# A two-layer encoder on one core: seven first-stage tiles with k outermost, x by chunks, the squares' adds on VectorE and the first norm ahead of the last chunk's products

## The chip, the cores and the metric

The kernel runs on one core of one Trainium2 chip. The metric is the time of one execution on the device in microseconds (us); less is better. A profiled execution also has a span, from its first to its last instruction. TensorE (PE) multiplies matrices, VectorE (DVE), ScalarE (ACT) and GpSimd (POOL) work element by element, and SyncE (SP) issues DMA transfers. PEld is TensorE's weight load, which runs beside its matmuls.

## The reference

All arrays are float32. `x` is 256 tokens of width 1024. Each of two layers computes, from `h = rms_norm(x)`, one wide product `h @ w_in`, whose columns feed three mixers and their gates: latent attention ("a": latents of 256 and 128 columns and a rotary part of 32), dilated attention ("b") and neighbourhood attention ("c": q, k and v of 8 heads of 64). The mixers' outputs are gated, go through an output product and are added to `x`; then comes a SwiGLU feed-forward of width 2816 on a second norm. A last norm ends the kernel. Cut to what bears on the change:

```python
def rms_norm(x, g):
    xf = x.astype(jnp.float32)
    y = xf * lax.rsqrt(jnp.mean(xf * xf, axis=-1, keepdims=True) + EPS)
    return (y * g.astype(jnp.float32)).astype(x.dtype)
...
    q = (rms_norm(c_q, g_q) @ w_uq).reshape(B, S, MLA_HEADS, MLA_NOPE_DIM + MLA_ROPE_DIM)
    kv = (rms_norm(c_kv, g_kv) @ w_ukv).reshape(B, S, MLA_HEADS, MLA_NOPE_DIM + MLA_V_DIM)
```

The norm's factor is a number per token, so the kernel multiplies the plain `x * g` with the weights and applies the factor `RB` to the products afterwards. The latents `c_q` and `c_kv` have norms of their own, which must be finished before their products with `w_uq` and `w_ukv` can start.

## The kernel before, in words

**Layout.** Channels lie on the 128 partitions, so `x` is 8 chunks of 128 channels by 256 tokens in `X`. Every float32 operand is used as a rounded part and a remainder: `prep` makes `XH` (ACT) and `XL` (DVE) of a chunk of `x * g`. A weight chunk is loaded by SP into a `raw` buffer (6 buffers, five chunks ahead), `split_next` makes `hi` of it on ACT and `lo` on DVE (4 buffers each), and `mm3` uses it in three matmuls of 256 columns a tile: hi with XH, hi with XL, lo with XH. `plan` fixes the order of the weight chunks, and `take` hands out the next one and starts the split of the one after it.

**First stage (key "a").** For each k of the 8 channel chunks: `prep`, one weight chunk of 640 columns, and five tiles' products, 15 matmuls; two of the tiles are the first half of the neighbourhood keys ("ck"). After every second chunk `square_pair` squares two chunks on ACT; POOL adds the squares up. After the loop `rstd` sums them over the channels (matmuls into `ps_ss`), takes the inverse root (`newton`, on ACT and DVE), and spreads it over the partitions (`ps_r`, then a copy into `RB`). Then `cq`, `ckv` and their squares are made, the other two "ck" tiles are multiplied (`n_tile`, 24 matmuls each), and the latent norm follows: sums in `ps_n`, `newton_wide` (two Ln and one Exp on ACT; two multiplications and a last step on DVE, lines 378 to 380), multiplications on POOL (L729, L730), then `chl`: rounded part on ACT (L735), remainder on DVE (L736). Four "cq" tiles, a "cv" tile and "cvk" products lie beside it; they do not need `chl`. `latent_q` (chunks "uq") and `latent_kv` ("ukv") do. After them `latent_rope` makes 16 small multiplications on DVE (L764), and six "b" q tiles come next.

**Feed-forward start.** `residual`, `prep` of two chunks, one "f" weight chunk, `square_pair` and 24 matmuls into `ps_f`, four times; `lo` of the first "f" chunk is made on POOL, all others on DVE.

**Order.** The code names no order across tiles: the framework simulates the program when it is built and orders each engine's instructions by readiness and free buffers. So the order within an engine changes where code, sizes or engines change; each engine then runs its list strictly in order. Matmuls of several stages stand mixed in TensorE's list.

Of the kernel before, what the change touches and what calls it, by code (L numbers as in the profile page):

```python
# [18 lines left out]
S = 256  # L19
NL = 2  # L20
KC = D // P
# [74 lines left out]

def plan():

    out = [(("a", k), 640) for k in range(KC)]
    out += [(("ck", i), 1024) for i in (2, 3)] + [(("cq", i), 1024) for i in range(4)]  # L100
    out += [(("uq", 0), 768)] + [(("cv", 0, h), 1024) for h in range(2)] + [(("uq", 1), 768)]
    for k, n in LAST:
        out += [(("cvk", k, n), 288 * n)] + [(("ukv",), 1024)] * (k == 0)
    out += [(("b", "q", i), 1024) for i in range(6)]
    out += [(("bv", 0, q), 1024) for q in range(4)] + [(("bv", 2, h), 1024) for h in range(2)]
    out += [(("b", "k", i), 1024) for i in range(6)]
    out += [(("g", j, br), 1024) for j in range(8) for br in range(3)]
    for j in range(10):
        if j < 8:
            out += [(("mab", j), 768), (("mc", j), 512)]  # L110
        if j > 1:
            out += [(("o", j - 2), 1024)]
    out += [(("f", c), 1024) for c in range(4)]
    for f in range(2, NF):
        out += [(("w1", f), 1024), (("w3", f), 1024)]
        if f > 2:
            out += [(("w2", f - 3), 1024)]
    out += [(("w2", f), 1024) for f in range(NF - 3, NF)]
    return out
# [6 lines left out]
def pack_weights(i, l):  # L126
# [17 lines left out]
    def part(key):  # L144
        n = key[0]
        if n == "a":
            c = np.concatenate([np.arange(384), nb_heads("ck", 0), nb_heads("ck", 1)])
            return w_in[P * key[1] : P * key[1] + P, c]
        if n in ("ck", "cq"):
            return tiles(w_in, nb_heads(n, key[1]))  # L150
        if n == "cvk":
            c = np.concatenate([OFF_C + 1280 + np.arange(256), 384 + n32])
# [40 lines left out]
    out = []  # L193
# [38 lines left out]
def f32(ap):  # L232
    return ap.bitcast(F32)
# [3 lines left out]
def encoder(ctx: ExitStack, tc: tile.TileContext, x, w, gains, cst, rpb, gfin, out):  # L237
# [52 lines left out]
    def split_next():  # L290
        i = at["split"]
        width = chunks[i][2]
        t = raw.pop(i)
        hi = ring.tile([P, 1024], F32R, tag="hi", name="hi", bufs=4)
        lo = ring.tile([P, 1024], F32R, tag="lo", name="lo", bufs=4)
        act.copy(hi[:, :width], t[:, :width])  # L296
        eng = pool if chunks[i][1] == ("f", 0) else dve
        ins = eng.tensor_sub(lo[:, :width], t[:, :width], f32(hi[:, :width])).ins  # L298
        if eng is dve and "hold" in at:
            queue(ins, at["hold"])  # L300
        split[i] = (hi, lo)
        at["split"] += 1
# [100 lines left out]
    def square_pair(c2):  # L403
        xs = X[:, 2 * c2 : 2 * c2 + 2, :].rearrange("p c s -> p (c s)")
        if c2 == 0:
            t = tmp.tile([P, 2, 512], F32, tag="qb", name="sqs", bufs=1)
            sqs["t"] = t[:, 0, :]
            act.activation(sqs["t"], xs, AF.Square)
        else:
            q = tmp.tile([P, 512], F32, tag="t2k", name="sq", bufs=4)  # L410
            act.activation(q, xs, AF.Square)
            pool.tensor_add(sqs["t"], sqs["t"], q)

    def sums(ps, at, sq, n, col, start):

# [197 lines left out]
    if True:  # L613
# [5 lines left out]
        for i in range(10):  # L619
            mm(wb, warm[:, :P], warm, True, True)  # L620
        act.dma_start(G, gains)
        ahead(0, 1)
        sp.dma_start(X[:, 1, :], x[:, 1, :])
        for c2 in range(1, 4):
            ahead(0, c2 + 1)
            sp.dma_start(X[:, 2 * c2 : 2 * c2 + 2, :], x[:, 2 * c2 : 2 * c2 + 2, :])

        def load_consts(n):
            return sp.dma_start(C[:, CPARTS[n] : CPARTS[n + 1]], cst[:, CPARTS[n] : CPARTS[n + 1]])
# [17 lines left out]
        for l in range(NL):  # L647

            gq, gk = bank("pv", "ps_g"), bank("pv", "ps_g")
            pc = [bank("g", "ps_g"), bank("g", "ps_g")]  # L650
            for k in range(KC):
                prep(k, GM + 8 * l)
                wt = take(l, "a", k)
                if k % 2:
                    square_pair(k // 2)
                for n in range(5):
                    o = (gq, gk, pc[0])[(n + n // 3) // 2][:, cols((n + n // 3) % 2, S)]
                    mm3(o, wt, cols(n), XH[:, k, :], XL[:, k, :], k == 0 and n in (0, 2, 3), k == 7)
            if l == 0:
                load_consts(0)  # L660
            rstd()


            QA = tmp.tile([P, 8, S], F32, tag="qa", name="QA", bufs=1)
# [46 lines left out]
                    stack(v, [QC[e][:, n, :] for e in range(2)], [v.bitcast(F32R)] * 2, "lo")  # L711

            c_out("k", 0, pc[0])
            for i in range(2):
                n_tile(l, pc[1][:, cols(i, S)], ("ck", 2 + i))
            c_out("k", 1, pc[1])
            if l == 0:
                braw = bias_tile()
# [272 lines left out]
            for c2 in range(4):  # L991
# [5 lines left out]
                for kk in range(2):  # L997
                    k = 2 * c2 + kk
                    for n in range(4):
                        mm3(fb[n // 2][:, cols(n % 2, S)], wt, slice(kk * 512 + n * P, kk * 512 + n * P + P),  # L1000
                            XH[:, k, :], XL[:, k, :], k == 0 and n % 2 == 0, k == 7)

            def swiglu(o):
                ab = tmp.tile([P, 2, S], F32, tag="t2k", name="fab", bufs=4)
                dve.tensor_mul(ab, o.rearrange("p (n s) -> p n s", n=2), bc(RB, 2))  # L1005
                halves["s"] = 4 - halves.get("s", 0)
                s = SG[:, halves["s"] : halves["s"] + 3, :]
                fn(s[:, 0, :], ab[:, 0, :], AF.Sigmoid)
                pool.tensor_mul(s[:, 1, :], ab[:, 0, :], ab[:, 1, :])  # L1009
                dve.tensor_mul(s[:, 2, :], s[:, 1, :], s[:, 0, :])  # L1010
                lag.append(in_halves(s[:, 2, :]))
# [123 lines left out]
```

## Time and profile before

| | us |
|---|---|
| median of 3 runs | 920.01 |
| the runs | 917.07, 920.01, 2275.41 |
| the profiled execution | 919.51 |
| its span | 917.7 |

The profiled execution's time is 1.8 us more than its span and 0.5 us under the median of the runs. The mean granted TensorE clock is 0.996 of full speed. Busy time is the time in which an engine had an instruction under way; the sum of a group's durations can be larger where instructions overlap. For matmuls that follow one another, the distance of their starts is the price of one, and not the duration shown, which has the pipeline's fill in it.

### The profile page before, as it was taken

To read this page: it belongs to the slowest core of one execution; us is meant where nothing else is said; L and a number is where in the kernel's file an instruction comes from. 1 tells how busy PE (TensorE), PEld (TensorE's weight loads), DVE (VectorE), ACT (ScalarE), POOL (GpSimd) and SP (SyncE) were. 2 spreads that over 40 slices of the span, in tenths; PEclk is the share of its full clock that TensorE was granted. 3 is DMA by queue.
4 is the path that set the end of the run, shared out by engine and by line. 5 is a ranking of instruction groups with operands and counts; after the bars stand their busy time and mean duration, and the time that the engine had idled before them with its cause. 6 is when DMAs were issued, how large, how long until landed. Compare 5 with 4: busy or idle time off the path is not lost.

```text
span 917.7 us, 18370 instructions
## 1 busy us (share of the span) xinstructions
PE 903.4 (98%) x7350; PEld 864.8 (94%) x7350; DVE 660.2 (72%) x1003; ACT 520.2 (57%) x858; POOL 127.4 (14%) x138
## 2 busy tenths in 40 slices
PE   8999999999999999999999999999999999999996
PEld 6999899999999999999999979999999999999995
DVE  6989876555888666666699898665577976666663
ACT  6687974544656444444477789545355654444443
POOL 2223013000022100000023230400000210000000
PEclk9999999999999999999999999999999999999998
DMA  8985455444666765665377654543456566555531
GB/s 284 292 280 187 135 154 173 118 136 144 203 205 199 260 207 185 190 190 187 110 239 213 222 159 137 154 139 133 129 182 219 166 211 203 185 184 189 197 120 46
DMA packets 53030, 166.70 MB, mean 182 GB/s; under 512 B 6352, under 2 KB 7120, under 8 KB 52944
## 3 DMA queue, kind: packets, MB, share of 16 engines
q1 hardware_dynamic: 48384, 158.69, 53.8%
q0 software_dynamic: 1920, 3.15, 1.6%
q10 hardware_dynamic: 2640, 3.69, 1.1%
q8 instruction: 58, 0.95, 0.4%
q14 instruction: 28, 0.23, 0.1%
HBM read 157.64 MB, written 1.05 MB: 173 GB/s over the span
## 4 chain that ended last, share of the span: by engine, by line
PE 93%; DVE 4%; ACT 1%; DMA 1%; issue 0%; SPq 0%; DVEq 0%
PE ps_g L322 63%; PE ps_acc L322 16%; PE ps_s L322 3%; PE ps_y L322 3%; PE ps_t L522 2%; PE ps_c L322 2%; DVE lo L298 2%; PE ps_f L322 1%; PE ps_a L322 1%; DVE XL L399 1%; DMA X<-in_x 1%; ACT hi L296 1%; DVE t L975 0%; DVE X L987 0%; PE ps_r L322 0%
## 5 line engine op out<-in xcount | busy, mean ns | idle before, releaser
L296 ACT CAST hi<-raw 128x1024 fp32r<-128x1024 f32 (+5 forms) x308 | 304.3, 993 | 311.6 <-PE ps_g L322 160.2
L298 DVE TENSOR_TENSOR lo<-raw,hi 128x1024 fp32r<-128x1024 f32 (+4 forms) x306 | 372.8, 1226 | 143.2 <-ACT hi L296 142.2
L322 PE MATMUL ps_g<-XH,hi 128*128 128x256 f32 x1392 | 392.2, 283 | 1.1 <-ACT hi L296 1.1
L322 PE MATMUL ps_g<-XL,hi 128*128 128x256 f32 x1392 | 389.6, 281 | 0.0
L322 PE MATMUL ps_g<-XH,lo 128*128 128x256 f32 x1392 | 386.3, 280 | 1.6 <-DVE lo L298 1.6
L322 PEld LDWEIGHTS ps_g<-XH,hi 128*128 128x128 f32 x1392 | 261.8, 188 | 5.4 <-issue 1.9
L322 PEld LDWEIGHTS ps_g<-XL,hi 128*128 128x128 f32 x1392 | 262.2, 188 | 3.2 <-issue 2.3
L322 PEld LDWEIGHTS ps_g<-XH,lo 128*128 128x128 f32 x1392 | 260.4, 188 | 2.4 <-DVE lo L298 2.2
L322 PE MATMUL ps_acc<-HL,hi 128*128 128x256 f32 x608 | 109.3, 280 | 0.0
L322 PEld LDWEIGHTS ps_acc<-HL,hi 128*128 128x128 f32 x608 | 93.1, 188 | 0.0
L322 PE MATMUL ps_acc<-HL,lo 128*128 128x256 f32 x304 | 84.2, 279 | 0.0
L1009 POOL TENSOR_TENSOR SG<-fab 128x256 f32<-128x256 f32 x44 | 34.5, 786 | 305.7 <-DVE fab L1005 302.5
L322 PEld LDWEIGHTS ps_acc<-HL,lo 128*128 128x128 f32 x304 | 57.1, 188 | 0.0
L322 PE MATMUL ps_acc<-hi,HL 128*128 128x512 f32 x176 | 55.3, 395 | 0.0
L1005 DVE TENSOR_TENSOR fab<-ps_g,RB 128x512 f32<-128x512 f32 x40 | 27.6, 691 | 22.2 <-PE ps_g L322 22.2
L322 PE MATMUL ps_g<-hi,XH 128*128 128x256 f32 (+2 forms) x128 | 40.4, 316 | 0.0
L322 PE MATMUL ps_g<-hi,XL 128*128 128x256 f32 (+2 forms) x128 | 40.0, 313 | 0.0
L322 PE MATMUL ps_g<-lo,XH 128*128 128x256 f32 (+2 forms) x128 | 39.9, 315 | 0.0
L322 PEld LDWEIGHTS ps_acc<-hi,HL 128*128 128x128 f32 x176 | 31.7, 188 | 6.1
L322 PE MATMUL ps_acc<-lo,HL 128*128 128x512 f32 x88 | 34.8, 395 | 0.0
L532 ACT COPY pT<-ps_t 128x512 f32<-128x512 f32 (+1 forms) x48 | 26.1, 549 | 14.1 <-PE ps_t L522 13.8
L926 DVE TENSOR_TENSOR GL<-ps_g,RB 128x512 f32<-128x512 f32 x20 | 13.8, 692 | 24.0 <-PE ps_g L322 24.0
(194 smaller groups left out, 1247.1 us busy)
## 6 DMA issues: line engine op xcount, KB each, us to landing
raw<-in_w SPq DMA_DIRECT2D x250, 512.0 KB, 3.6
raw<-in_w SPq DMA_DIRECT2D x20, 384.0 KB, 3.1
raw<-in_w SPq DMA_DIRECT2D x16, 320.0 KB, 3.3
braw<-in_rpb SPq DMA_DIRECT2D x16, 256.0 KB, 5.1
raw<-in_w SPq DMA_DIRECT2D x16, 256.0 KB, 2.8
t<-t ACTq DMA_DIRECT2D x24, 128.0 KB, 3.2
raw<-in_w SPq DMA_DIRECT2D x4, 432.0 KB, 4.2
KCt<-KCt POOLq DMA_DIRECT2D x8, 128.0 KB, 5.1
```

The source lines that it names most:

```text
L296: act.copy(hi[:, :width], t[:, :width])
L298: ins = eng.tensor_sub(lo[:, :width], t[:, :width], f32(hi[:, :width])).ins
L322: pe.matmul(o, a, b, start=start, stop=stop, skip_group_check=True)
L399: dve.scalar_tensor_tensor(out=XL[:, c, :], in0=X[:, c, :], scalar=g, in1=f32(XH[:, c, :]), op0=ALU.mult, op1=ALU.subtract)
L522: pe.transpose(u.tr[:, cols(k)], u.p[:, cols(k)], cc("ident"))
L532: act.copy(u.pT[:, :n], u.tr[:, :n])
L926: dve.tensor_mul(d0[:, n0 : n0 + 2, :], o.rearrange("p (n s) -> p n s", n=2), bc(RB, 2))
L1005: dve.tensor_mul(ab, o.rearrange("p (n s) -> p n s", n=2), bc(RB, 2))
L1009: pool.tensor_mul(s[:, 1, :], ab[:, 0, :], ab[:, 1, :])
```

## The change

The change makes the first stage's chunk 896 columns wide, with all four "ck" tiles in it: seven tiles and 21 matmuls a chunk, and no separate "ck" tiles after it. The second "ck" bank comes from the tag "acc". `x` is loaded in single chunks of 128 KB, each after a weight chunk's transfer; the constants are asked for at k = 3 and not after the loop. The adds of the squares go to DVE as one function, `add_squares`; `rstd` is called before the last chunk's products are emitted; at the feed-forward `add_squares` is called after the loop. `lo` of the first "f" chunk is made on DVE.

```diff
@@ def plan
-    out = [(("a", k), 640) for k in range(KC)]
-    out += [(("ck", i), 1024) for i in (2, 3)] + [(("cq", i), 1024) for i in range(4)]
+    out = [(("a", k), 896) for k in range(KC)]
+    out += [(("cq", i), 1024) for i in range(4)]
...
@@ def split_next
-        eng = pool if chunks[i][1] == ("f", 0) else dve
-        ins = eng.tensor_sub(lo[:, :width], t[:, :width], f32(hi[:, :width])).ins
-        if eng is dve and "hold" in at:
+        ins = dve.tensor_sub(lo[:, :width], t[:, :width], f32(hi[:, :width])).ins
+        if "hold" in at:
...
@@ def square_pair
-            sqs["t"] = t[:, 0, :]
+            sqs["t"], sqs["more"] = t[:, 0, :], []
             act.activation(sqs["t"], xs, AF.Square)
         else:
             q = tmp.tile([P, 512], F32, tag="t2k", name="sq", bufs=4)
             act.activation(q, xs, AF.Square)
-            pool.tensor_add(sqs["t"], sqs["t"], q)
+            sqs["more"].append(q)
+
+    def add_squares():
+        for q in sqs["more"]:
+            dve.tensor_add(sqs["t"], sqs["t"], q)
...
@@ the loads of x
-        ahead(0, 1)
-        sp.dma_start(X[:, 1, :], x[:, 1, :])
-        for c2 in range(1, 4):
-            ahead(0, c2 + 1)
-            sp.dma_start(X[:, 2 * c2 : 2 * c2 + 2, :], x[:, 2 * c2 : 2 * c2 + 2, :])
+        for c in range(1, KC):
+            ahead(0, min(c, 6))
+            sp.dma_start(X[:, c, :], x[:, c, :])
...
@@ the first stage
-            pc = [bank("g", "ps_g"), bank("g", "ps_g")]
+            pc = [bank("g", "ps_g"), bank("acc", "ps_g")]
             for k in range(KC):
                 prep(k, GM + 8 * l)
                 wt = take(l, "a", k)
+                if l == 0 and k == 3:
+                    load_consts(0)
                 if k % 2:
                     square_pair(k // 2)
-                for n in range(5):
-                    o = (gq, gk, pc[0])[(n + n // 3) // 2][:, cols((n + n // 3) % 2, S)]
-                    mm3(o, wt, cols(n), XH[:, k, :], XL[:, k, :], k == 0 and n in (0, 2, 3), k == 7)
-            if l == 0:
-                load_consts(0)
-            rstd()
+                if k == KC - 1:
+                    add_squares()
+                    rstd()
+                for n in range(7):
+                    o = (gq, gk, *pc)[(n + (n > 2)) // 2][:, cols((n + (n > 2)) % 2, S)]
+                    mm3(o, wt, cols(n), XH[:, k, :], XL[:, k, :], k == 0 and n in (0, 2, 3, 5), k == 7)
...
             c_out("k", 0, pc[0])
-            for i in range(2):
-                n_tile(l, pc[1][:, cols(i, S)], ("ck", 2 + i))
             c_out("k", 1, pc[1])
...
@@ the feed-forward, after the loop over c2
+            add_squares()
```

**How the order moves.** DVE at the latent norm of layer 0, before (the `nw` and `R_` rows are `newton_wide`; `lo` rows split weight chunks, told apart by width: 1024 for "cq", "cv" and "ukv", 768 for "uq", 864 and 576 for "cvk"):

```order
L378 TENSOR_TENSOR nw<-nw,R_427 128x512
L710 SCALAR_TENSOR_TENSOR cv<-ps_g,RB 128x512
L379 TENSOR_TENSOR nw<-nw,R_427 128x512
L298 TENSOR_TENSOR lo<-raw,hi 128x1024
L380 SCALAR_TENSOR_TENSOR R_427<-nw,R_427 128x512
L439 TENSOR_TENSOR cv<-cv,QC 64x512 x2
```

And the same place now:

```order
L377 TENSOR_TENSOR nw<-nw,R_418 128x512
L442 TENSOR_TENSOR cv<-cv,QC 64x512 x2
L378 TENSOR_TENSOR nw<-nw,R_418 128x512
L442 TENSOR_TENSOR cv<-cv,QC 64x512 x2
L297 TENSOR_TENSOR lo<-raw,hi 128x864
L379 SCALAR_TENSOR_TENSOR R_418<-nw,R_418 128x512
```

Four remainders of the "cq" tiles and an 864-wide split now stand inside the three steps of the latent norm; a multiplication and one 1024-wide split stood there before.

ACT at the same place, before and now (the `R_` rows are the norm's Ln, Ln and Exp):

```order
L344 ACTIVATE R_427<-ps_n,C 128x256
L296 CAST hi<-raw 128x768
L344 ACTIVATE R_427<-ps_n,C 128x256
L344 ACTIVATE R_427<-R_427 128x512
L296 CAST hi<-raw 128x1024
```

```order
L343 ACTIVATE R_418<-ps_n,C 128x256 x2
L296 CAST hi<-raw 128x768
L343 ACTIVATE R_418<-R_418 128x512
L441 CAST QC<-cv 64x512 x4
L296 CAST hi<-raw 128x864
```

The 768-wide cast was that of "uq" 0 and stood between the two Ln; now it is that of "uq" 1, behind both and ahead of the Exp.

TensorE where `chl` is first read, before and now, with buffer numbers (`hi_549` is "uq" 0, `hi_589` a "cv" chunk; now `hi_540` is "uq" 0, `hi_640` "uq" 1, `hi_673` the first "cvk"):

```order
L322 MATMUL ps_g_617<-hi_589,XH_68 128x256
L322 MATMUL ps_a_596<-chl_437,hi_549 128x256
L322 MATMUL ps_r_588<-chl_437,hi_549 128x256
L322 MATMUL ps_g_617<-hi_589,XL_69 128x256
L322 MATMUL ps_g_617<-lo_590,XH_68 128x256
```

```order
L321 MATMUL ps_g_717<-hi_673,XL_69 128x288
L321 MATMUL ps_g_717<-lo_674,XH_68 128x288
L321 MATMUL ps_a_587<-chl_428,hi_540 128x256
L321 MATMUL ps_r_579<-chl_428,hi_540 128x256
L321 MATMUL ps_a_680<-chl_428,hi_640 128x256
L321 MATMUL ps_g_718<-hi_673,XH_68 128x288
```

The first reader of `chl` stood among the "cv" products; now it stands behind all of them and behind nine "cvk" matmuls.

DVE at the rotary step, before and now:

```order
L298 TENSOR_TENSOR lo<-raw,hi 128x864
L764 TENSOR_TENSOR QA<-ps_r,C 32x256 x16
L298 TENSOR_TENSOR lo<-raw,hi 128x576
L298 TENSOR_TENSOR lo<-raw,hi 128x1024 x6
```

```order
L297 TENSOR_TENSOR lo<-raw,hi 128x864
L297 TENSOR_TENSOR lo<-raw,hi 128x576
L765 TENSOR_TENSOR QA<-ps_r,C 32x256 x16
L297 TENSOR_TENSOR lo<-raw,hi 128x1024 x5
```

The last "cvk" split has moved from behind the 16 multiplications to ahead of them.

## Rows read from the trace of the kernel before

**Rows 1.** The page's first part: busy time, share of the span and instructions of each engine.

```profile
PE 903.4 (98%) x7350; PEld 864.8 (94%) x7350; DVE 660.2 (72%) x1003; ACT 520.2 (57%) x858; POOL 127.4 (14%) x138
```

**Rows 2.** The waits of TensorE over the span: what waited, for what, us in all, times, longest.

```profile
PE ps_f L322 <- DVE XL L399: 2.0, 2, 1.0
PE ps_g L322 <- DVE lo L298: 1.6, 3, 0.5
PE ps_g L322 <- ACT hi L296: 1.1, 1, 1.1
```

**Rows 3.** Busy time by stretch: the stretch, its length, busy us (instructions) of PE, PEld, DVE, ACT, POOL, then the granted TensorE clock, the DMA engines' share and GB/s.

```profile
0.00:20.00 20.00, 16.12 (x99) 12.69 (x99) 12.75 (x18) 13.16 (x22) 6.76 (x9) 1.00 0.82 280
4.00:5.00 1.00, 1.00 (x3) 0.30 (x2) 0.48 (x1) 0.64 (x2) 0.00 (x0) 1.00 1.04 350
34.00:60.00 26.00, 26.00 (x218) 25.97 (x217) 24.44 (x40) 20.30 (x31) 6.36 (x9) 1.00 0.87 270
60.00:120.00 60.00, 60.00 (x456) 53.97 (x455) 52.13 (x110) 48.37 (x110) 13.51 (x16) 1.00 0.55 172
```

**Rows 4.** TensorE's timeline at the start, in the "cvk" products and at the feed-forward of layer 0: start, duration, engine, line, operation, what was idle before it and for whom.

```profile
1.21 4.45 PE L322 MATMUL warm<-warm 128*128 128x512 bf16 x10 [1.21 <-DVE warm L617]
5.67 0.41 PE L322 MATMUL ps_g<-XL,hi 128*128 128x256 f32 x1
5.88 0.41 PE L322 MATMUL ps_g<-XH,hi 128*128 128x256 f32 x1
...
7.46 0.28 PE L322 MATMUL ps_g<-XH,hi 128*128 128x256 f32 x1
7.57 0.28 PE L322 MATMUL ps_g<-XL,hi 128*128 128x256 f32 x1
...
10.78 0.39 PE L322 MATMUL ps_g<-XH,hi 128*128 128x256 f32 x1 [1.06 <-ACT hi L296]
...
58.02 0.30 PE L322 MATMUL ps_g<-hi,XL 128*128 128x288 f32 x1
58.15 0.29 PE L322 MATMUL ps_g<-lo,XH 128*128 128x288 f32 x1
...
278.69 0.38 PE L322 MATMUL ps_f<-XL,hi 128*128 128x256 f32 x1 [1.00 <-DVE XL L399]
```

**Rows 5.** The chain of waits from the first norm's sums to the first reader of `chl`, layer 0: start, us, what.

```profile
19.45 0.79 PE ps_ss L322 x8
20.23 6.06 PE ps_g L322 x51
26.29 0.44 PE ps_r L322 x4
26.74 6.78 PE ps_g L322 x58
33.52 0.86 PE ps_n L322 x4
34.38 11.24 PE ps_g L322 x96
45.62 0.11 PE ps_a L322
```

**Rows 6.** ACT's timeline, columns as in Rows 4.

```profile
4.36 0.72 ACT L296 CAST hi<-raw 128x640 fp32r<-128x640 f32 x1 [0.39 <-DMA raw<-in_w]
...
34.79 0.83 ACT L296 CAST hi<-raw 128x768 fp32r<-128x768 f32 x1
36.20 0.63 ACT L344 ACTIVATE R<-R 128x512 f32<-128x512 f32 x1
42.50 0.91 ACT L735 ACTIVATE chl<-QA,G 128x256 fp32r<-128x256 f32 x2 [1.31 <-POOL QA L729]
48.43 1.20 ACT L755 ACTIVATE QA<-ps_a 64x512 f32<-64x512 f32 x2 [0.89 <-PE ps_a L322]
53.54 0.67 ACT L296 CAST hi<-raw 128x576 fp32r<-128x576 f32 x1
```

**Rows 7.** DVE's timeline, columns as in Rows 4.

```profile
9.23 0.89 DVE L399 SCALAR_TENSOR_TENSOR XL<-X,G,XH 128x256 fp32r<-128x256 f32 x2 [1.45 <-ACT XH L398]
12.15 1.91 DVE L399 SCALAR_TENSOR_TENSOR XL<-X,G,XH 128x256 fp32r<-128x256 f32 x2
...
25.90 1.23 DVE L298 TENSOR_TENSOR lo<-raw,hi 128x1024 fp32r<-128x1024 f32 x1 [0.54 <-ACT hi L296]
35.69 0.96 DVE L298 TENSOR_TENSOR lo<-raw,hi 128x768 fp32r<-128x768 f32 x1
37.09 0.69 DVE L378 TENSOR_TENSOR nw<-nw,R 128x512 f32<-128x512 f32 x1
47.27 1.40 DVE L439 TENSOR_TENSOR cv<-cv,QC 64x512 fp32r<-64x512 f32 x2
48.70 1.06 DVE L298 TENSOR_TENSOR lo<-raw,hi 128x864 fp32r<-128x864 f32 x1
52.97 6.93 DVE L764 TENSOR_TENSOR QA<-ps_r,C 32x256 f32<-32x256 f32 x16
```

**Rows 8.** POOL's timeline at the latent norm and at the feed-forward of layer 0, columns as in Rows 4.

```profile
40.87 1.59 POOL L729 TENSOR_TENSOR QA<-QA,R 128x512 f32<-128x512 f32 x1 [6.72 <-DVE R L380]
276.61 3.17 POOL L412 TENSOR_TENSOR sqs<-sqs,sq 128x512 f32<-128x512 f32 x2 [1.95 <-ACT sq L411]
```

More of the change, by code (lines that the diff above doesn't have):

```diff
@@ L146, in part @@
         if n == "a":
-            c = np.concatenate([np.arange(384), nb_heads("ck", 0), nb_heads("ck", 1)])
+            c = np.concatenate([np.arange(384)] + [nb_heads("ck", t) for t in range(4)])
             return w_in[P * key[1] : P * key[1] + P, c]
-        if n in ("ck", "cq"):
+        if n == "cq":
             return tiles(w_in, nb_heads(n, key[1]))
```

## The prediction

> **What bounds the kernel now.** First the page's busy times: TensorE is busy for 98% of the span, DVE for 72%, POOL for 14% [rows 1]. Only about 14 us of the span are not TensorE's, so the most that better feeding can give is small, and what the change can lose is any idle time that it opens on TensorE. Then TensorE's waits: two at the feed-forward's start for XL, 2.0 us together, and four in front of first-stage products, 1.6 for `lo` and 1.1 for `hi` [rows 2]. Third, the stretches: in the first 20 us TensorE is busy for 16.1 with DVE and ACT at 13; from 34 to 60 us it is busy throughout, but DVE is at 24.4 of 26 us, and from 60 to 120 at 52.1 of 60 [rows 3]. So the stage of the latent norm is one in which DVE has almost no room, and TensorE does not wait there only because it has other products to run meanwhile. The chain of waits shows that cover: from the start of `ps_ss` at 19.45 to the first reader of `chl` at 45.62 all is TensorE's own work, 26.2 us [rows 5]. The change shortens just this stretch, since two "ck" tiles move from behind the first norm's sums to ahead of them.
>
> The price of a matmul is the distance of starts: 0.11 at 7.46 and 7.57 [rows 4], 0.117 as the mean of 96 in 11.24 us [rows 5], which I take; 0.13 for 288 columns (58.02, 58.15) [rows 4]; 0.21 at the start (5.67, 5.88) [rows 4].
>
> **The change, part by part, against the profiled 919.51 us** (0.5 under the median, 1.8 over its span).
>
> *First stage, gain.* Six more matmuls a chunk (21 for 15, 2.46 us for 1.76) give ACT and DVE longer per chunk, and POOL's add leaves: the pair of XL that took 1.91 us at 12.15 took 0.89 at 9.23 [rows 7]. DVE then needs per chunk 0.45 for XL and some 1.1 for an 896-wide `lo` (between the 864-wide, 1.06, and the 1024-wide, 1.23 [rows 7]), and 0.69 for an add in three of eight chunks (the size of line 378's multiplication [rows 7]): 1.55 to 2.24 under 2.46 of TensorE. That work hides the adds; without it each costs its 0.69. So the four waits go, 2.7 us [rows 2], with a restart of 0.1 each (the first matmul after an idle time lasts 0.39, others 0.28 [rows 4]): **-3.1**. Bounds: 0, if transfers are the limit (rival B), and -3.1.
>
> *First stage, cost.* The first chunk has 256 more columns: 128 KB at 350 GB/s [rows 3] is 0.37, and its `hi` cast is longer, 0.72 for 640 columns and 0.83 for 768 [rows 6], so 0.94 for 896, 0.22 more. The first real matmul comes 0.6 later: **+0.6**. Matmuls and weight bytes are the same in sum.
>
> *Feed-forward start.* POOL's adds, 3.17 us for two at 276.61 [rows 8], leave, and XL is no longer stretched. TensorE came free at 277.69 and got its XL at 278.69, 1.00 us late [rows 4]. Now the pair of XL ahead of it on DVE is 1.0 shorter (0.89 for 1.91 [rows 7]), an add of 0.69 comes in front, and the XL itself is 0.5 shorter: 0.8 earlier and, with what an XL waits for POOL at its start, just in time. `lo` of the first "f" chunk, 1.23, stands in front of the last gated product, under dense products. Both waits go, 2.0 and 0.2 for restarts: **-2.2**. Bounds: 0 and -2.2. The adds after the loop, 2.1 us, are hidden by the first "w1" tile, 2.8 us, after which the sums stand.
>
> *Latent norm, a new wait.* Time runs from the start of `ps_ss`. TensorE's own work up to the first reader of `chl` is now, by the new order and the prices above: `ps_ss` 0.79, 35 products 4.10, `ps_r` 0.44, 60 products 7.02, `ps_n` 0.86 (its end is at 13.2), 70 products 8.19, nine of 288 columns 1.20: **22.6**, for 26.2 before. The chain to `chl`: after 13.2 ACT does both Ln, then the cast of "uq" 1, and this cast needs a `hi` buffer that is free when the last "cq" tile's 22 left matmuls are done, 2.58, at 15.8; cast 0.83 [rows 6], 16.6. Exp (0.63 [rows 6]) waits behind it, so the norm waits for a weight buffer: 17.3. DVE meanwhile ends the 768-wide `lo` (0.96 [rows 7]) at 17.6. Then, in the new order, multiplication 0.69, two remainders 1.40, multiplication 0.69, two remainders 1.40, the 864-wide `lo` 1.06 and the norm's last step 0.69 [rows 7]: 23.5. POOL 1.59 [rows 8]: 25.1. ACT's first half of the pair, 0.46 of 0.91 [rows 6]: 25.6. TensorE is there at 22.6 and has nothing else: its next products stand behind, and the four `hi` buffers hold "uq" 0, "uq" 1, the first "cvk" and "ukv", of which three need `chl`. Wait: 25.6 - 22.6 = **3.0 in each of two layers**. Bounds: 0 (in the trace `chl` was made from 42.50 [rows 6], 2.7 us ahead of its reader at 45.62 [rows 5]; the shorter cover alone takes 3.6), and 5 if the parts wait for one another. I take the worked chain, as its order is that of the program.
>
> *Rotary step, a second wait.* The last `ps_r` product comes 47 matmuls, 5.6 us, after TensorE resumes. ACT makes the first QA pair from 4.0 to 5.2 (1.20), then the 576-wide cast (0.67 [rows 6]) to 5.9; DVE its `lo`, about 0.7 by width, to 6.6. Only then come the 16 multiplications, 6.93 [rows 7], to 13.5, and the 1024-wide `lo` of the first "b" q tile, 1.23 [rows 7], to 14.7. TensorE wants that `lo` at 12.4: 69 matmuls at 0.117 and 32 of 288 columns at 0.133. Before, the 576-wide split stood behind the 16. Wait: **2.3 in each layer**; bounds 0 and 3.
>
> *The clock during the waits.* The granted clock reads 1.00 in the stretches shown [rows 3], but the first products start 0.21 apart, the lower of the two levels, 1.2 GHz, and 0.11 apart from 7.46 on [rows 4], the higher one, 2.4 GHz. After the idle 1.06 us before 10.78 [rows 4] the stage still does all its work at the higher price. No wait of before is as long as 3.0 us. By the rows I count no loss of clock. If it falls for a stretch like that at the start, from 1.21 to about 6.7 us, half of 5.5 us is lost: 2.75 each time. The Trainium skill ("TensorE: Matmul & The Clock Gate", section "HAM oscillation — how this bites in real kernels") says that idle gaps between bursts of matmuls bring the clock back to the lower level; by it the two longer waits would cost 2 x 2.75 and the sum would be 5.5 us higher. The 1.06 us gap does not show it, and no run here has a longer one.
>
> **Sum:** +0.6 - 3.1 - 2.2 + 2 x 3.0 + 2 x 2.3 = +5.9, so 919.5 + 5.9 = **925.4 us**.
>
> **Rivals.**
>
> *A, the cover is enough.* The framework's order is what I read, but the "cq" remainders and the QC copies may be ready when DVE gets there, buffers may come free earlier, and the trace had 2.7 us of room at `chl`. Then only the gains are left: 919.5 + 0.6 - 3.1 - 2.2 = **914.8**. For it: in 34 to 60 us TensorE never waited [rows 3]. Against it: DVE had 1.6 us free there in 26, and the cover is 3.6 shorter. Chance 0.25.
>
> *B, the first stage stays bound by its transfers,* so the change does not do there what it says. A chunk with its piece of `x` is 576 KB in 2.46 us, 240 GB/s, against 280 on average and 350 at best in this stage [rows 3]; the rows speak against it, the many small pieces ahead of the weights for it. Then the 3.1 isn't gained: **928.5**. Chance 0.15. The Trainium skill ("DMA: Bandwidth & Descriptors", section "Measured (HBM→SBUF") gives less bandwidth to smaller transfers, which speaks for this rival; no row here has x in pieces of this kind side by side with pairs.
>
> *C, the other side: the clock falls in the new waits.* As above, at `chl` in both layers, the place where TensorE is idle longest. It decides once an idle time of about 3 us is enough. 925.4 + 5.5 = **930.9**. Chance 0.10.
>
> **The numbers.** The forecast has 0.50; its own range is 921 to 929 (waits of half to one and a quarter of what I worked out, and the runs' scatter). About 2%, 18.4 us, is what a measurement of this kernel can tell from no change. Slower by that would need more than three times the waits: 0.03. Faster by that would need more than TensorE's whole idle time of 14 us: 0.01. Within: 0.96. The range for 8 in 10 takes in A and most of B and C: 913 to 931.
>
> **What would show it.** Right: in the first stage TensorE's waits for `hi` and `lo` are gone, `ps_f` waits for no XL, a wait of `ps_a` for `chl` of about 3 us stands in both layers some 23 us after `ps_ss`, with the three steps of the latent norm spread over 6 us of DVE, and the first "b" q tile waits about 2 us for a `lo` behind the 16 multiplications. The parts can be wrong one by one: no wait at `chl` is A; waits on `raw` in the first stage are B; products 0.21 apart behind the wait are C. All is wrong if the norms' Ln and Exp, now early, hold TensorE at the sums `ps_ss` or `ps_r`, or if some later stage, where the order has moved too, opens waits that I did not price.

## The result, and the profile after

The changed kernel takes 932.54 us (median of 4 runs, 931.26 to 933.59), the kernel before 919.77 in the same session (one of its four runs took 2275 us and is left out of the ratio): a ratio of 1.0145, 95% interval 1.0132 to 1.0157. It is slower by 12.8 us and lies 1.5 us above the range of the prediction. The profiled execution has 933.59 us, a span of 931.8 and a mean granted clock of 0.991 (0.996 before).

The page's busy times first; they answer to [rows 1].

```profile
PE 910.0 (98%) x7350; PEld 870.6 (93%) x7350; DVE 654.4 (70%) x1013; ACT 518.8 (56%) x854; POOL 106.0 (11%) x124
```

TensorE is busy 6.6 us longer with the same 7350 matmuls: some of them ran slower. Its waits (what waited, for what, us in all, times, longest) answer to [rows 2]:

```profile
PE ps_g L321 <- DVE lo L297: 5.7, 4, 2.3
PE ps_a L321 <- ACT chl L736: 4.4, 2, 2.2
...
PE ps_g L321 <- DVE cv L713: 1.2, 2, 0.8
PE ps_g L321 <- ACT hi L296: 0.6, 1, 0.6
```

The waits for XL at the feed-forward and the four first-stage waits are gone, as forecast. New are 2.2 us at `chl` and 2.3 us for the `lo` behind the rotary step, in each layer, as forecast, and 0.6 for another `lo` (the first "cvk" remainder) and 0.4 and 0.8 for a bank (`cv`), which were not. The 0.6 for `hi` is ahead of the first product. TensorE's timeline at both places of layer 0 shows what follows a wait:

```profile
46.83 0.40 PE L321 MATMUL ps_g<-lo,XH 128*128 128x288 f32 x1 [0.56 <-DVE lo L297]
...
47.73 0.29 PE L321 MATMUL ps_g<-lo,XH 128*128 128x288 f32 x1
50.23 0.39 PE L321 MATMUL ps_a<-chl,hi 128*128 128x256 f32 x1 [2.21 <-ACT chl L736]
...
50.73 0.44 PE L321 MATMUL ps_g<-hi,XH 128*128 128x288 f32 x1
50.97 0.44 PE L321 MATMUL ps_g<-hi,XL 128*128 128x288 f32 x1
...
64.19 0.28 PE L321 MATMUL ps_g<-XL,hi 128*128 128x256 f32 x1
66.80 0.38 PE L321 MATMUL ps_g<-XH,lo 128*128 128x256 f32 x1 [2.33 <-DVE lo L297]
...
67.75 0.41 PE L321 MATMUL ps_g<-XH,hi 128*128 128x256 f32 x1
67.96 0.41 PE L321 MATMUL ps_g<-XL,hi 128*128 128x256 f32 x1
```

Half a microsecond after TensorE resumes at 50.23, products of 288 columns stand 0.24 apart, and not 0.13 as in [rows 4]; after the second wait, products of 256 stand 0.21 apart. The stretches (columns as in [rows 3], the granted clock is the number before the DMA share) show the clock fall to half, the lower of its two levels, 1.2 GHz, and return:

```profile
49.00:50.00 1.00, 0.00 (x0) 0.00 (x0) 0.00 (x0) 0.33 (x1) 1.00 (x2) 1.00 1.01 406
50.00:51.00 1.00, 0.77 (x5) 0.77 (x6) 0.78 (x2) 0.98 (x3) 0.33 (x1) 0.82 0.99 407
51.00:52.00 1.00, 1.00 (x6) 1.00 (x6) 0.50 (x2) 0.00 (x0) 0.00 (x0) 0.50 0.96 376
...
54.00:55.00 1.00, 1.00 (x10) 1.00 (x10) 1.00 (x1) 0.00 (x0) 1.00 (x2) 0.98 0.01 4
```

From 50 to 55 us the clock column lacks 0.18 + 0.5 + 0.5 + 0.5 + 0.02 = 1.7 us of full speed. The same sum at the other three places (67 to 72, 508 to 512, 525 to 530) is 1.7 each: 6.8 in all. What this cost in time is read from the starts: a product of 256 columns takes 0.213 at half the clock, which is less than twice 0.117, and in layer 1 the clock had fallen at 508.0, half a microsecond before TensorE resumed at 508.53. Above the full-speed distances the four stretches cost 1.5, 1.5, 1.4 and 1.6 us, 6.0 in all.

Where the 14.1 us of span come from is read by counting matmuls from 0, 7350 in both traces. The start of the 100th moves from 20.30 to 17.05, so the first stage wins 3.25; the 260th from 39.35 to 35.66, -3.7; the 380th, behind `chl`, from 53.49 to 55.88, +2.4; from the 500th on, behind the rotary step, the change is 6.4 behind. The first feed-forward gives 1.0 back (5.46 at the 2600th), layer 1 loses 9.7 (15.15 at the 5000th), with no first-stage wait to win, and from there to the end 1.1 comes back, with the last feed-forward in it: 14.0.

What holds `chl` is seen on DVE; its timeline of the change at the latent norm:

```profile
41.65 0.68 DVE L377 TENSOR_TENSOR nw<-nw,R 128x512 f32<-128x512 f32 x1
42.25 1.40 DVE L442 TENSOR_TENSOR cv<-cv,QC 64x512 fp32r<-64x512 f32 x2
43.68 0.69 DVE L378 TENSOR_TENSOR nw<-nw,R 128x512 f32<-128x512 f32 x1
44.29 1.40 DVE L442 TENSOR_TENSOR cv<-cv,QC 64x512 fp32r<-64x512 f32 x2
45.72 1.06 DVE L297 TENSOR_TENSOR lo<-raw,hi 128x864 fp32r<-128x864 f32 x1
46.70 0.68 DVE L379 SCALAR_TENSOR_TENSOR R<-nw,R 128x512 f32<-128x512 f32 x1
```

The three steps of the norm are spread from 41.65 to 47.4, as the order had said; `chl` is first read at 50.23, 26.4 us after the sums (`ps_ss` starts at 23.87), for 25.6 in the prediction.

### The profile page after: what moved, and what is told of

Same layout as the page of the kernel before. It is cut to its first block, busy times and chain, and to the rows that moved or that the text cites. A ratio compares the mean times of both kernels' runs of the same rounds, so it can differ in the third digit from the quotient of the medians.

```text
span 931.8 us, 18339 instructions
## 1 busy us (share of the span) xinstructions
PE 910.0 (98%) x7350; PEld 870.6 (93%) x7350; DVE 654.4 (70%) x1013; ACT 518.8 (56%) x854; POOL 106.0 (11%) x124
## 4 chain that ended last, share of the span: by engine, by line
PE 94%; DVE 3%; ACT 1%; issue 1%; POOL 0%; DMA 0%; SPq 0%; ACTq 0%; POOLq 0%
PE ps_g L321 62%; PE ps_acc L321 17%; PE ps_s L321 3%; PE ps_y L321 3%; PE ps_c L321 2%; PE ps_f L321 2%; PE ps_t L525 2%; DVE lo L297 1%; PE ps_a L321 1%; ACT hi L296 1%; DVE QA L765 1%; POOL QA L730 0%; DMA raw<-in_w 0%; PE ps_r L321 0%; PE ps_ss L321 0%
## 5 line engine op out<-in xcount | busy, mean ns | idle before, releaser
L296 ACT CAST hi<-raw 128x1024 fp32r<-128x1024 f32 (+4 forms) x304 | 304.0, 1003 | 332.1 <-PE ps_g L321 178.6
L1008 DVE TENSOR_TENSOR fab<-ps_g,RB 128x512 f32<-128x512 f32 x40 | 27.6, 691 | 22.1 <-PE ps_g L321 22.1
L520 DVE TENSOR_SCALAR p<-p,m 128x256 f32<-128x256 f32 (+1 forms) x80 | 33.3, 450 | 1.6
L535 ACT COPY pT<-ps_t 128x512 f32<-128x512 f32 (+1 forms) x48 | 26.4, 550 | 14.0 <-PE ps_t L525 13.6
```

The lines of the kernel that those rows point to most:

```text
L520: dve.tensor_scalar_mul(u.p[:, ps], u.p[:, ps], u.m[:, 2 + hh : 3 + hh])
L535: act.copy(u.pT[:, :n], u.tr[:, :n])
```

## The experiments

Each kernel was run beside the kernel before on the same chip; ratios are to it. A difference to the change is one between medians of two sessions, so it is clear of the noise only where the two intervals lie apart. First, the change with one part undone.

**e1_ck_behind.** The two last tiles stand behind the norm again:

```diff
-    out = [(("a", k), 896) for k in range(KC)]
+    out = [(("a", k), 640) for k in range(KC)]
+    out += [(("ck", i), 1024) for i in (2, 3)]
...
-                for n in range(7):
+                for n in range(5):
...
+            for i in range(2):
+                n_tile(l, pc[1][:, cols(i, S)], ("ck", 2 + i))
             c_out("k", 1, pc[1])
```

> The change with one part undone: the two last "ck" tiles stand behind the first norm again (640-wide chunks, five tiles a chunk); the adds on VectorE, the early norm and x by chunks stay. Theory (the tiles moved ahead of the norm took TensorE's cover away): by the program's order the work between the first norm's sums and the first reader of chl is 24.6 us in layer 0 and 25.1 in layer 1, for 21.4 and 21.1 with the change; chl takes about 26 from the sums, so its wait of 2.2 falls below 1 in both layers and the clock holds there. In layer 1 the rotary step again has 75 matmuls behind it and its wait goes, in layer 0 it has 57 and stays with its clock loss, about 4. Sum 917 to 921 us. Rival 1 (VectorE, loaded with the adds, is what is late) and rival 2 (the early norm reorders the engines) leave all four waits: 929 to 933.

Measured: 919.35 us, ratio 1.0003 (0.9994 to 1.0012). TensorE's waits:

```profile
PE ps_g L322 <- DVE lo L298: 1.9, 2, 1.7
...
PE ps_g L322 <- ACT hi L297: 0.6, 1, 0.6
PE ps_r L322 <- DVE dg L388: 0.5, 1, 0.5
PE ps_a L322 <- DVE chl L740: 0.3, 1, 0.3
```

With the tiles behind the norm, `chl` is in time in both layers (0.3 once), and one rotary wait of 1.7 is left, in layer 0. The seven tiles are what cost 13 us; that they cost it by the cover that they took away is the reading that e10_cvk_first, below, bears out. Two things differ from the expectation: no low clock followed the rotary wait, and one (1.2 us lost, from 23.2 to 25.7 us) followed two short gaps at 20.5 and 21.6, the first for a `hi`, the second in front of `ps_r`.

**e2_rstd_behind.** The norm behind the loop again, seven tiles kept:

```diff
-                if k == KC - 1:
-                    add_squares()
-                    rstd()
...
+            add_squares()
+            rstd()
```

> The change with one part undone: add_squares and rstd stand behind the whole loop again; seven tiles and the adds on VectorE stay. Theory (cover): the sums start 21 matmuls, 2.5 us, later against the same work, so the cover behind them is 18.9 us for 21.4; what of it reaches chl depends on the slack in front of the second norm: the waits at chl grow by 0 to 2.5 in each layer, 933 to 938 us. Rival 2 (the early norm is what disturbs the order): the waits go and the time is near that of before, 917 to 921.

Measured: 941.02 us, 1.0239 (1.0215 to 1.0263), slower still by 8.5 than the change. TensorE's waits:

```profile
PE ps_g L321 <- DVE lo L297: 10.2, 4, 2.8
PE ps_g L321 <- DVE cv L709: 6.0, 2, 3.1
```

The direction is that of cover, the size is above the range: beside longer waits for `lo` there is a new one of 3 us in each layer for `cv`, the step that frees the bank of the next tile and itself needs `RB`. The clock falls four times here, and once, from 497.4 to 504.2, it stays low for twice as long as in the change. So the early emission of the norm is a help; it gives back 21 of the 48 matmuls that moved in front.

**e3_adds_pool.** The adds on POOL again:

```diff
-            dve.tensor_add(sqs["t"], sqs["t"], q)
+            pool.tensor_add(sqs["t"], sqs["t"], q)
```

> The change with one part undone: the squares' adds on POOL again. The order at both norms is nearly that of the change. Theory: the adds on VectorE have nothing to do with the new waits; all eight stretches (chl, rotary step, low clock) stay, and the feed-forward's two waits for XL of about 1.0 come back: 933 to 936. Rival (the adds load VectorE and so make the new waits): the waits shrink, below 931.

Measured: 933.35 us, 1.0157 (1.0140 to 1.0174). The waits at `chl` (4.4 us for two) and for `lo` are those of the change. The clock falls at three of the four places and not at all four: the rotary wait of layer 0 (2.59 between starts at 65.38) has no fall behind it, and the fall at `chl` of layer 0 lasts from 49.3 to 56.2, with 2.7 us lost. The waits for XL are back at 1.3 us for two, less than before. The adds have no part in the new waits.

**e6_before_dve_adds.** The other way round: the kernel before with the adds on DVE alone (the diff of e3, reversed).

> The kernel before with one part of the change alone: the squares' adds on VectorE, everything else as before. Theory (this part is a gain by itself, as forecast): the two waits of 1.0 for XL at the feed-forward go with their restarts, 2.2 us, and of the four first-stage waits, 3.1 us, some part goes, since an XL takes 0.45 and not 0.95 but an add of 0.69 stands on VectorE; 914 to 917.5. Rival (the adds load VectorE where it is short): 919 or more.

Measured: 915.55 us, 0.9969 (0.9957 to 0.9980). This part of the change is a gain by itself, 0.3% and clear of the noise. One first-stage wait is left, on TensorE's timeline:

```profile
11.23 0.39 PE L322 MATMUL ps_g<-XH,hi 128*128 128x256 f32 x1 [1.51 <-ACT hi L296]
```

Next, the mechanism at `chl`.

**e4_norm_first.** No work changed, only rules of order, which put the norm's steps ahead on ACT and DVE:

```diff
+        if chunks[i][1] == ("uq", 1):
+            queue(cast, at["exp"])
...
+        if chunks[i][1] == ("uq", 1) or chunks[i][1][:2] == ("cvk", 0):
+            queue(ins, at["norm"])
...
+            if hold:
+                queue(ins, at["norm"])
```

> The change, with ordering rules alone: the cast of "uq" 1 stands behind the second norm's Exp on ACT, and the "cq" remainders, the "uq" 1 remainder and the first "cvk" remainder stand behind the norm's three steps on VectorE. No work is changed. Theory (the chain to chl is stretched by 3.9 us of other work inside the norm on VectorE): the norm's last step ends about 4 us earlier, chl waits less than 1 us, no low clock behind it; the waits and the low clock at the rotary step stay. 2 x (2.2 + 1.7), about 8 us, are saved: 922 to 927. Rival (only the cover counts, the order on VectorE does not matter): 931 to 934.

Measured: 933.94 us, 1.0160 (1.0145 to 1.0175): nothing is won. My theory of the order was wrong. DVE's timeline:

```profile
42.20 0.69 DVE L384 SCALAR_TENSOR_TENSOR R<-nw,R 128x512 f32<-128x512 f32 x1
42.81 2.38 DVE L447 TENSOR_TENSOR cv<-cv,QC 64x512 fp32r<-64x512 f32 x2
45.22 1.39 DVE L299 TENSOR_TENSOR lo<-raw,hi 128x768 fp32r<-128x768 f32 x1
46.53 1.40 DVE L447 TENSOR_TENSOR cv<-cv,QC 64x512 fp32r<-64x512 f32 x2
47.96 1.06 DVE L299 TENSOR_TENSOR lo<-raw,hi 128x864 fp32r<-128x864 f32 x1
```

The norm's last step ends at 42.9 and not at 47.4, and `chl` is ready more than four microseconds earlier. But the work that was put behind it ends at 49.0, and the first "cvk" remainder, now its last, is what TensorE waits for (1.5 us between starts at 47.55; 3.1 in layer 1), behind a wait of 0.7 for a `hi`. DVE has the same list to get through, but my rules did not put it in the order of need: the four "cq" remainders, 2.8 us, stand ahead of that "cvk" remainder (the rows at 42.81 and 46.53), and TensorE first reads what comes of them at 72.66:

```profile
72.66 0.36 PE L325 MATMUL ps_s<-KCt,QC 128*128 128x256 f32 x1
```

An order with the "cvk" remainder ahead of the four was not run.

**e13_no_q_remainders.** So the list was made shorter:

```diff
-            dve.tensor_sub(lo[e][r], src[r], f32(d[e][r]))
+            if not skip:
+                dve.tensor_sub(lo[e][r], src[r], f32(d[e][r]))
```

> The change without the subtraction that makes the remainder of the "c" q halves: four instructions of 0.7 us a layer fewer on VectorE, between the steps of the second norm; the other half of QC then holds q itself and not its remainder. Everything else stands in the order of the change. Theory (the amount of work that VectorE has between the first norm and the reader of chl is the limit, not its order, as e4_norm_first made another remainder late): chl and the first "cvk" remainder come 2.8 earlier, their waits (2.2 and 0.6 with their restarts) and the low clock behind go in both layers, about 9 us: 922 to 925; the rotary wait stays. Rival (the chain is held by ACT's casts or by POOL): less than 3 us saved, 929 to 933.

Measured: 926.02 us, 1.0075 (1.0060 to 1.0090), 6.5 less than the change, a little short of the forecast. The waits at `chl` shrink to 0.3 once, the low clock there is gone, the rotary waits (2.3) and the low clock behind them stay. So the four remainders, where they stand, are what holds `chl`: the rival, ACT or POOL, is out. Whether it is the amount of DVE's work or its order is not shown: the four are first read some 25 us later, so putting them behind the "cvk" remainder might have won the same as leaving them out.

**e7_fill.** TensorE busy in the wait for `chl`, nothing moved:

```diff
+            fb1 = bank("pv", "fill")
+            for j in range(5):
+                mm(fb1[:, :S], cc("ones"), R23[:, 0, :], True, True)
             latent_q(0)
```

> The change plus five dummy float32 products of 256 columns (about 0.43 us each) on TensorE, which read the second norm's result and write a bank that nobody reads, in the place of the wait for chl, both layers; so TensorE is busy in most of that wait and nothing else is moved. Theory (the clock falls because TensorE is idle there): chl comes as late as before, but the products behind it run 0.117 apart and not 0.21; 1.7 us a layer are won, 928 to 930 us, and the low clock remains behind the rotary step alone. Rival (the clock falls for another reason, such as the engines' or the transfers' load at that place): products behind chl 0.21 apart as before, 932 to 934.

Measured: 929.41 us, 1.0113 (1.0098 to 1.0128), 3.1 less than the change. TensorE's timeline, and one stretch of it:

```profile
47.58 2.32 PE L321 MATMUL fill<-R,C 128*128 128x256 f32 x10
49.95 0.39 PE L321 MATMUL ps_a<-chl,hi 128*128 128x256 f32 x1
...
50.41 0.29 PE L321 MATMUL ps_g<-hi,XH 128*128 128x288 f32 x1
50.54 0.30 PE L321 MATMUL ps_g<-hi,XL 128*128 128x288 f32 x1
```

```profile
51.00:52.00 1.00, 1.00 (x10) 1.00 (x10) 0.21 (x1) 0.34 (x1) 0.00 (x0) 1.00 0.83 294
```

The five products are ten matmuls in the trace, 0.22 apart. `chl` is read at the same distance behind the "cvk" products as in the change, but the products behind it stand 0.13 apart and the clock stays at 1.00. So it is TensorE's idleness that takes the clock down there, and that is worth about 1.5 us each time, 3.1 for two; all four runs (929.2 to 929.8) lie below the change's fastest, 931.26. What I did not foresee: in this run the rotary wait of layer 0, 2.48 us between starts, was followed by no fall, and that of layer 1, 2.47, was.

Then the rotary step, and whether the seven tiles can be kept.

**e5_rope_split.** Ten of the 16 multiplications where they stood, six behind the remainders of the first two "b" q tiles:

```diff
-            latent_rope()
+            latent_rope(range(10))
...
                         n_tile(l, o[:, cols(i, S)], ("b", w_, 2 * i2 + i))
+                        if w_ == "q" and i2 == i == 0:
+                            latent_rope(range(10, 16))
```

> The change, with the rotary step on VectorE cut in two: ten of its 16 multiplications where they stood, the last six behind the remainders of the first two "b" q tiles. Same work. Theory (TensorE waits there only for a remainder that stands behind all 16, and the low clock follows from that wait): the waits of 2.3 to 2.5 at the first "b" q tile and the low clock of 1.55 behind them go in both layers, about 8 us: 923 to 926; the waits and the low clock at chl stay. Rival (VectorE is behind with all its work, so the wait only moves to the next tile): 929 to 933.

Measured: 930.95 us, 1.0138 (1.0120 to 1.0156): 1.6 less than the change by the medians, with intervals that overlap. The rotary wait is gone, but TensorE now waits 1.1 and 0.7 in each layer for `kr`, a step of POOL in front of `ps_k`. In layer 0 no low clock follows these waits, in layer 1 one does, from 528.5 to 531.9; the wait at `chl` of layer 1, 2.50 between starts at 503.91, has none behind it this time. The rival is nearer: the wait moved.

**e10_cvk_first.** All "cvk" products ahead of the readers of `chl`, and the rotary step in four groups:

```diff
-    out += [(("uq", 0), 768)] + [(("cv", 0, h), 1024) for h in range(2)] + [(("uq", 1), 768)]
-    for k, n in LAST:
-        out += [(("cvk", k, n), 288 * n)] + [(("ukv",), 1024)] * (k == 0)
+    out += [(("cv", 0, h), 1024) for h in range(2)] + [(("cvk", k, n), 288 * n) for k, n in LAST]
+    out += [(("uq", 0), 768), (("uq", 1), 768), (("ukv",), 1024)]
...
+                        if w_ == "q" and i2 < 2:
+                            latent_rope(range(8 * i2 + 4 * i, 8 * i2 + 4 * i + 4))
```

> The change with its seven tiles, and cover given back by other work: all "cvk" products stand ahead of the readers of chl (39 more matmuls, 5.2 us, between the first norm's sums and chl: 26.5 us), and the 16 rotary multiplications stand in four groups behind the remainders of the "b" q tiles. Same work. Theory (cover is what the change lost, whatever supplies it): no wait over 1 us at chl or at the "b" q tiles, no low clock, all of the change's gains kept: 913 to 918, faster than before. Rival (VectorE's total work in this stretch is the limit, in whatever order): a wait of 2 us or more stands elsewhere in the stretch and the time is 922 or more.

Measured: 920.65 us, 1.0022 (1.0012 to 1.0033), between the two forecasts. The cover works: no wait at `chl`, and at the 520th matmul the kernel is 3.5 us ahead of the one before. Then one wait stands in each layer, with a low clock behind it, here on TensorE's timeline of layer 0:

```profile
73.26 0.58 PE L321 MATMUL ps_g<-XH,hi 128*128 128x256 f32 x1 [2.17 <-DVE t L867]
```

It is for a bank that DVE's line 867 frees, and DVE worked almost without a gap from 57 us on to get there (14.6 of the 15 us to 72). This is the rival's sign.

**e12_cvk_rope_late.** The same with the rotary step later:

```diff
-                        if w_ == "q" and i2 < 2:
-                            latent_rope(range(8 * i2 + 4 * i, 8 * i2 + 4 * i + 4))
+                        if w_ == "q":
+                            latent_rope(range(*([(0, 0), (0, 2), (2, 4), (4, 6), (6, 10), (10, 16)][2 * i2 + i])))
```

> e10_cvk_first with the rotary step later: none behind the first "b" q tile, then groups of 2, 2, 2, 4 and 6 multiplications. Theory (in e10_cvk_first the step that frees the "b" q bank, line 867, stood behind all 16 on VectorE; ten of them are now ahead of it): the wait of 2.2 there falls below 1 and the low clock goes, in both layers, 2 x 3.5 us: 912 to 916, faster than the kernel before and than the adds alone. Rival (VectorE is out of time in the whole stretch to 80 us): the wait appears one or two tiles later, 918 or more.

Measured: 919.76 us, 1.0005 (0.9996 to 1.0014): no low clock any more, but waits of 0.66 and 0.25 for line 867 in each layer, in layer 0 up to 72.6 and 79.7 us, and the lead of 3.6 at the 560th matmul has fallen to 1.4 at the 800th. The rival's time and sign are met: what the seven tiles win in the first stage of layer 0 is mostly lost in the stretch behind, and layer 1, with nothing to win, loses 3.2 more between the 3600th and the 5000th. That DVE's debt is the reason is my reading: the two waits for its line 867 account for 1.3 of the 2.2 us, between starts, and the rest lies in gaps that I did not trace.

Last, the parts that help, without the seven tiles.

**e9_adds_x_rope.** e1_ck_behind with `rstd` behind the loop and the rotary step cut as in e5_rope_split.

> e1_ck_behind with the norm behind the loop again, as in the kernel before, and the rotary step cut in two as in e5_rope_split; what is left of the change is the adds on VectorE and x by chunks. Theory: against e1_ck_behind the two early waits of layer 0 (0.8 and 0.8 between starts, 1.3 lost), the low clock behind them (1.2) and the rotary wait of layer 0 (1.9) go: 914 to 916, faster than both kernels. Rival (the early norm gave e1_ck_behind its cover, and without it chl waits again): 918 or more.

Measured: 924.34 us, 1.0058 (1.0040 to 1.0076), a miss. TensorE, now 4.1 us ahead at the 80th matmul, overtakes the first norm: gaps of 1.4 and 1.1 between starts at 20.4 and 22.1 (for `hi` and for `ps_r`) and a low clock behind them take the lead away, and the cut rotary step brings the wait for `kr` here too, again with a low clock behind it in layer 0. Layer 1 loses 4 us more, 2.5 of them in waits for `kr`, `AH` and `VB`. `chl` did not wait, so it was not the rival's reason either.

**e17_adds_x1.** e6_before_dve_adds with the second pair of x loaded as two chunks:

```diff
-        for c2 in range(1, 4):
+        ahead(0, 2)
+        sp.dma_start(X[:, 2, :], x[:, 2, :])
+        sp.dma_start(X[:, 3, :], x[:, 3, :])
+        for c2 in range(2, 4):
```

> e6_before_dve_adds (the adds on VectorE alone) with chunks 2 and 3 of x loaded singly and not as a pair of 256 KB, the rest as before. Theory (the one long first-stage wait that is left there, 1.5 us for hi, comes from the pair of x that lands 6.5 us after its issue): that gap of 1.8 between starts shrinks below 0.5, the cover behind the first norm's sums stays that of the kernel before (24.7 us by the order): 913 to 915.5. Rival (the stage is short of transfers or of ACT, so that the time comes back at the next chunk, or the earlier start makes ps_r wait as in e9_adds_x_rope): 915.5 or more.

Measured: 914.48 us, 0.9952 (0.9939 to 0.9966), in the range: faster than both kernels, by 0.5% than the kernel before. The gap shrank from 1.79 to 0.59 between starts, not quite below 0.5. The interval overlaps that of e6_before_dve_adds, so the gain over the adds alone is clear in the trace (spans of 912.5 and 913.8) but not in the times. All that is left of TensorE's waits:

```profile
PE warm L322 <- DVE warm L617: 1.2, 1, 1.2
PE ps_g L322 <- ACT hi L296: 0.3, 1, 0.3
```

## Why the prediction was wrong

**Right: the two new waits and their place.** Forecast were 3.0 at `chl` and 2.3 at the rotary step in each layer. Measured between starts, less the 0.12 or 0.13 of a matmul: at `chl` 2.4, with 0.7 for the "cvk" remainder and 0.5 (layer 1: 1.0) for the bank of `cv` in front of it, 3.6 and 4.1; at the rotary step 2.5 and 2.4. So `chl` was undersized by 0.6 and 1.1: the chain came out at 26.4 for 25.6, and two stops in front of the reader were not priced. e1_ck_behind shows that the seven tiles are the cause, and e10_cvk_first that other cover in their place takes the wait at `chl` away.

**Right: the gains.** The first stage and its later start come to -3.25 for -2.5 forecast, the feed-forwards to -1.0 and -1.1 for -2.2 together. The first matmul came 1.1 later (5.13 to 6.25), not 0.6, yet at the 20th matmul, the ten of the warm-up counted, the lag was 0.5, since fewer products ran at the lower clock.

**Wrong: "By the rows I count no loss of clock."** This is the step that failed: the term was sized 0 and measured 6.8 by the clock column, 6.0 by the starts, at four places and not at two. It is most of the 8.2 between the sum (+5.9) and the span (+14.1); the undersized `chl` adds 1.7, the better first stage, with 0.4 more up to the 260th matmul, takes 1.2 off, the rotary waits add 0.3, and the 1.4 that are left lie in restarts, about 0.1 behind each wait, and in small gaps. The argument was a gap of 1.06 us that left the clock alone [rows 4]; it says nothing of one twice as long, and no such wait was in the trace. Rival C had the mechanism and, for two places, the price of 2.75 each; it got 0.10. That its 930.9 lay near the measured 932.5 is in part luck: 2 x 2.75 stood for four falls of about 1.5. The rule of the Trainium skill ("TensorE: Matmul & The Clock Gate", section "HAM oscillation — how this bites in real kernels"), that idle gaps between bursts bring the clock down, agrees with the change's trace in its direction: the granted clock goes from 1.00 to 0.50 at the waits of 2.2 to 2.3, and e7_fill keeps it at 1.00 by filling those at `chl`. The gaps that the section speaks of are longer than these, and here some waits of this length brought no fall.

**Also wrong: the margin.** Slower by 18.4 needs the waits at 2.2 times what I worked out, (18.4 + 4.7) / 10.6, and not at more than three times; and half to one and a quarter of them give 920.1 to 928.1, where I wrote 921 to 929.

**Half right: why `chl` is late.** I blamed the order inside the norm on DVE and a cast that waits for a buffer. e4_norm_first moved both, made `chl` four microseconds earlier and won nothing, since the work that it put off then held TensorE; e13_no_q_remainders removed work and won 6.5. That DVE's total between the first norm and the "b" q tiles is the limit, in any order, is argued and not shown: the order of need was not tried. The stretches show where DVE's time went: from 20 to 30 us it was busy for 8.2 of 10 us in the kernel before and is for 6.0 now.

```profile
20.00:30.00 10.00, 10.00 (x88) 10.00 (x88) 8.16 (x14) 5.93 (x10) 0.00 (x0) 1.00 0.97 349
```

```profile
20.00:30.00 10.00, 10.00 (x89) 10.00 (x88) 5.99 (x11) 4.95 (x7) 0.00 (x0) 1.00 0.76 281
```

The first row is the kernel before, the second the change (the third busy time is DVE). DVE's timeline of the change shows what it waited for there, and the third row, ACT's, why the first of these came late:

```profile
21.44 1.23 DVE L297 TENSOR_TENSOR lo<-raw,hi 128x1024 fp32r<-128x1024 f32 x1 [1.82 <-ACT hi L296]
25.02 0.16 DVE L358 TENSOR_SCALAR nt<-ps_ss 128x2 f32<-128x2 f32 x1 [2.36 <-ACT nt L343]
```

```profile
20.35 1.05 ACT L296 CAST hi<-raw 128x1024 fp32r<-128x1024 f32 x1 [2.51 <-DMA raw<-in_w]
```

It stood 1.8 us for the `hi` of a weight chunk that landed late, and 2.4 us at the first step of the first norm, whose sums TensorE starts only at 23.87 (19.45 before); what needs `RB` comes later still. Products that need nothing from DVE's backlog were used up ahead of the norm.

**Rivals A and B** are out: the cover was not enough, and no first-stage wait of TensorE for transfers is left. ACT's wait of 2.5 us for a chunk at 20.35, towards the end of that stage, shows that the transfers were not far from the limit there.

## What to carry to other kernels

When TensorE is busy all the time and another engine nearly so, products that need no result of that engine are a store of cover: spending them ahead of a norm leaves its chain bare, and moving the chain forward does not help when what TensorE needs next is put behind it. Price a new idle time of TensorE of two microseconds or more at its length and about 1.5 us on top, and give "the clock stays up" a chance, not a certainty, where the trace has no wait of that length. Try each part of a change alone: here one line, the adds on DVE, was worth 3.5 us, and the rest of the change hid it.

## What the runs showed of the hardware

In layer 0 of the change the clock's fall comes late and stays for a while: after the wait that ends at 50.23 the products slow down at 50.7 and are at full pace at 54.1; after the one that ends at 66.80 they are slow from 67.75 to 71.15, although TensorE is busy throughout. It can also come while TensorE still waits: at 508.0 in the change, with TensorE back at 508.53, and at 49.3 in e3_adds_pool, with TensorE back at 50.30. Nor does the length of one wait decide it. The traces of the change and of the experiments have 26 waits of two microseconds or more between starts; the clock fell at 18 of them. 2.48 us between starts at 62.40 in e7_fill cost nothing and 2.47 at 517.78 in the same run cost 1.6; 3.04 at 513.24 in e2_rstd_behind and 2.0 in e1_ck_behind cost nothing, while two gaps of 0.84 and 0.79 an instant apart did cost 1.2. What decides between them stays open.
